# Order of the front stage, index keys and look-ups of a hybrid encoder step: six edits to one kernel

## The chip, the core and the metric

The kernel runs on one core of one Trainium2 chip. The metric is the time of one execution on the device in microseconds (us). The profile is one execution recorded by the hardware profiler; its engines are PE (TensorE matmul), PEld (TensorE weight load, beside PE), DVE (VectorE), ACT (ScalarE), POOL (GpSimd) and SP (SyncE, whose queue issues most of the DMAs, in order).

## The reference

One layer for two groups of tokens that share weights: 8 sequences of 16 sample tokens with 256 cached tokens each, and one prompt of 256 tokens; 384 rows of 1024 in all. Cut to what matters here:

```python
h = rmsnorm(x) * (1 + scale1) + shift1            # mod = silu(c) @ w_ada + b_ada, six rows of 1024 per sequence
P_rw, P_dsa, P_gate = split(h @ w_in)             # 3360, 3656 and 2048 columns
o_a = rwkv7(P_rw)                                 # recurrence with a state per head, 16 heads of 64
q, k, v, qi, ki, wi = split(P_dsa)                # qi: 8 heads of 64, ki: one of 64, wi: 8
score = sum_h wi[h] * relu(rope(qi[h]) @ rope(ki).T)
idx = top_k(score, min(256, L // 4))              # 64 or 68 keys per query
o_b = softmax_attention(q, k[idx], v[idx])
ga, gb = split(sigmoid(P_gate + b_gate))
m = ga * (o_a @ w_proj_a) + gb * (o_b @ w_proj_b)
x = x + gate1 * (m @ w_out)
h2 = rmsnorm(x) * (1 + scale2) + shift2
# PEER: per head two top-16 lists out of 128 keys, 16 best of their pair sums, expert number from the two lists
s1, i1 = top_k(s[..., 0, :], 16); s2, i2 = top_k(s[..., 1, :], 16)
sc, j = top_k(pair_sums(s1, s2), 16); e = take(i1 * 128 + i2, j)
x = x + gate2 * sum(softmax(sc) * gelu(peer_u[e] @ h2) * peer_v[e])
```

Outputs are the new x, the recurrence states, the shifted rows, and k, v, ki.

## The kernel before, in words

**Matmuls.** Most projections hold each weight chunk as a rounded high part and a low part (`hilo`, line 225: ScalarE writes the high part, VectorE or GpSimd the difference, as `lo_pattern` says), and the activations `LT` too, and add three products. `wload` (line 240) loads 512 KB pieces through a ring of four `w` buffers into four `wh` and three `wl`. `natp` (line 261) holds 128 tokens and streams weight columns: 24 matmuls per token tile of 128. `tposp` (line 273) holds weight columns and streams all 384 tokens: 24 matmuls for up to 128 columns, result transposed. Both write one of two PSUM banks named `mm`.

**The front stage** (`run`, line 1550) is a list of units in the order of the string `ORDER` (line 177): `G` a gate unit (line 1130: 128 columns of the gate projection, sigmoid, stored to DRAM in `gd`; units 0 to 7 are branch A's gates, 8 to 15 branch B's), `I` the index unit, `R` one of eight recurrence pairs (line 524: two heads, three projections, then a long chain of small steps on all engines, result stored to `oad`), `D` one of four attention quarters (line 914: four heads, result to `obd`), `M` a modulation unit (line 379: 256 columns of `silu(c) w_ada`, full float32, row `mr` stored to DRAM).

The string gives priorities, not the final order: the builder simulates a time line and puts on each engine's queue, and on SP's, the earliest ready instruction. Rings and PSUM banks still follow one another in the order of use. Tile memory is in pools that open and close as stacks: `rw` for the pairs on one side, on the other first `idx` for the index unit and, when that is done, `dsa` for the quarters in the same place. A tile waits for the readers and writers of what lay there before.

**The index unit** (`index`, line 878) projects `qi` (two units of 256 columns) and then `ki` with `wi` (72 columns), all with `natp` via `nat3` (line 871), rotates them, transposes them, and calls `index_s` (line 990, sample scores, cached keys brought by SP) and `index_p` (line 961, prompt scores). `select` (line 953) finds the best keys by rounds of `max` (eight values) and `match_replace`, 9 for the sample tokens and 8 for each of two prompt tiles, on VectorE. The masks `mks`, `mkp` are its results; they lie outside `idx`.

**The mix** (`mix`, line 1146) reads `obd` back in four pieces (`parts`, line 1137), makes gate B x projection B (8 x `tposp`), then the same for `oad` and branch A, adds, and goes on to `w_out`, the second norm and `h2`. Its pool opens over memory of the front stage.

**Expert selection** (`peer_select`, line 1257), called twice with four heads for the sample tokens and twice with eight for the prompt tiles, runs on VectorE: top-16 lists, then a look-up of the chosen index numbers. The look-up (lines 1313 to 1324) compares positions with 0..15 (bf16, 1024 elements per partition), multiplies with the numbers, and sums over 16 places; only one of the 16 is not zero. There are 12 of these. `dense_u` (line 1433, PE) and `peer_sparse` (line 1514, gathers on GpSimd and products on VectorE) run beside it and after it; then come the expert weights and the dense products up to the end.

Of the kernel before, what the change touches and what calls it, by code (L numbers as in the profile page):

```python
# [12 lines left out]
F32 = mybir.dt.float32  # L13
# [163 lines left out]
ORDER = "GGIRRDMMMGRMRDMRGMGGMRMDGMMRRMGDMMMGGGGGGMGGM"  # L177
# [15 lines left out]
class K:  # L193
# [171 lines left out]
    def mod_head(self):  # L365
        nc = self.nc
        cT = self.t([128, 8, 9], tag="cT")
        nc.sync.dma_start(cT, self.I["cT"])
        sg = self.t([128, 8, 9], tag="cS")
        self.sigmoid(sg, cT)  # L370
        self.st = self.fconst.tile([128, 8, 32], F32, name="cst")
        nc.vector.memset(self.st, 0.0)
        nc.vector.tensor_tensor(self.st[:, :, 0:9], sg, cT, op=OP.mult)
        self.bcol = self.fconst.tile([128, 16], F32, name="bcol")
        nc.sync.dma_start(self.bcol, self.I["b_col"])
        self.modd = self.dt_([128, 6144])
        self.scT = self.fconst.tile([128, 2, 8, 9], F32, name="scT")

    def mod_unit(self, u):
# [7 lines left out]
        mr = self.t([128, 256], tag="mr", pool=self.fill)  # L387
# [64 lines left out]
    def front_h(self):  # L452
# [6 lines left out]
        self.h1A = self.fconst.tile([128, 8, 9], F32, name="h1A")  # L459
# [418 lines left out]
    def index(self):  # L878
        nc = self.nc
        H = lambda t: t.rearrange("p i (h d) -> p i h d", d=64)  # L880
        qiTs = self.t([64, 8, 8, 16], tag="qiTs")
# [16 lines left out]
        kiT = self.t([128, NT], tag="kiT")  # L898
        x = self.t([128, 3, 72], tag="qx")
        self.nat3("ki", x, 72)  # L900
        kr = self.t([128, 3, 2, 64], tag="qr")
        self.rope(kr[:, :, 0:1], x[:, :, 0:64].unsqueeze(2), 0, 1)
        nc.gpsimd.tensor_copy(kr[:, :, 1], kr[:, :, 0])
        nc.sync.dma_start(self.O["ki"].rearrange("(i p) c -> p i c", p=128), kr[:, :, 0])
        wi = self.t([128, 3, 8], tag="wi")
        nc.scalar.activation(wi, x[:, :, 64:72], AF.Copy, scale=512 ** -0.5)
        p = self.ps([128, 3, 128], tag="dx")
        for i in range(3):
            nc.tensor.transpose(p[:, i], kr[:, i].rearrange("p a b -> p (a b)"), self.ident)
        nc.scalar.activation(kiT, p.rearrange("p i t -> p (i t)"), AF.Copy)  # L910
# [235 lines left out]
    def mix(self):  # L1146
# [3 lines left out]
        for br, (src, w, tg) in enumerate(((self.obd, "w_proj_b", "pb"), (self.oad, "w_proj_a", "pa"))):  # L1150
            LT = self.parts(src, tg)
            if br:
                mh, ml = self.mT = [self.t([128, 8, NT], F32R, tag=tag) for tag in ("pbh", "pbl")]
            for u in range(4):
                W = self.wload(I[w][:, u], 256)
                for c in range(2):
                    k = 2 * u + c
                    g = self.t([128, NT], tag="gm", bufs=2) if br else gb[:, k]
                    nc.sync.dma_start(g, self.gd[8 - 8 * br + k])
                    p = self.tposp(W, c, 128, LT)  # L1160
                    nc.vector.tensor_tensor(g, g, p, op=OP.mult)
                    if br:
                        nc.gpsimd.tensor_tensor(g, g, gb[:, k], op=OP.add)
                        self.hilo(mh[:, k], ml[:, k], g, eng="v")
# [92 lines left out]
    def peer_select(self, i, h0=0, nh=8):  # L1257
# [57 lines left out]
        for half in range(2):  # L1315
            for h in range(0, nh, 4):
# [7 lines left out]
                nc.vector.tensor_reduce(out=idx[:, half, hs], in_=oh.rearrange("p h c k -> p h k c"), op=OP.add, axis=AX.X)  # L1324
# [225 lines left out]
    def run(self):  # L1550
        self.dense = False
        with ExitStack() as front:
# [20 lines left out]
            with ExitStack() as s:  # L1573
# [4 lines left out]
                for x in ORDER:  # L1578
# [6 lines left out]
                    self.pool = rw if x == "R" else ds  # L1585
                    {"R": self.rwkv_pair, "M": self.mod_unit, "G": self.gate_unit, "D": self.dsa_quarter}[x](n[x])
# [117 lines left out]
```

## Time and profile before

| | us |
|---|---|
| median of three runs (1849.57 to 1854.88) | 1850.84 |
| the profiled execution | 1852.01 |
| its span, first to last instruction | 1850.2 |

| stretch (us) | what runs |
|---|---|
| 0 to 60 | norm, first 8 modulation units, head of the recurrence |
| 60 to 142 | index projections and scores, first pairs |
| 142 to 186 | selection of keys, pairs 0 and 1 |
| 186 to 745 | pairs, quarters, modulation and gate units |
| 745 to 897 | mix, output projection, second norm |
| 897 to 1090 | expert selection, first dense products |
| 1090 to 1350 | more dense products, weights of the experts |
| 1350 to 1850 | dense and gathered products up to the output |

The busy share of an engine is an average over stretches with different limits; TensorE's busy time counts pipelined matmuls, so a busy PE need not run at its peak. [...] In rows of instructions an arrow in brackets names what ended the idle time before.

### The profile page before, as it was taken

The numbers are of one execution on the slowest core, as the hardware profiler recorded it, in microseconds if no ns is written. First come the engines' busy times: TensorE is split into PE (matmuls) and PEld (weight loads), VectorE is DVE, ScalarE is ACT, GpSimd is POOL, SyncE is SP. The second block draws the span as 40 slices with busy tenths as digits, with TensorE's granted clock in tenths as the row PEclk, the third lists the DMA queues.
The fourth block names the chain that finished last, engine by engine and source line by source line (L and its number), as shares of the span: only waits on it lengthen the run. The fifth ranks groups of instructions, "written<-read, shape, count | busy, mean of one in ns | idle before, by whom it ended". The sixth has DMA issues, their size and how long they took to land. (4 is left out here: it accounts for less than half of the span.)

```text
span 1850.2 us, 33639 instructions
## 1 busy us (share of the span) xinstructions
PE 1736.5 (94%) x12621; PEld 1434.4 (78%) x12621; DVE 1372.4 (74%) x2922; ACT 702.0 (38%) x1412; POOL 684.7 (37%) x751
## 2 busy tenths in 40 slices
PE   7997999999999989899999889999999989999998
PEld 4995788877887868698877779999975556677765
DVE  4549677877777755444999998899967787787783
ACT  4422343333343333333412145478842222333332
POOL 2321233232232210023244534554346675555541
PEclk7987999999999989899999999999999999999999
DMA  8421472454364264745478988976489999999994
GB/s 310 140 79 28 133 257 75 150 170 124 104 206 144 88 209 134 253 140 193 161 291 311 337 295 304 394 269 221 160 293 373 395 372 372 336 378 352 334 355 147
DMA packets 181083, 434.11 MB, mean 235 GB/s; under 512 B 39348, under 2 KB 78388, under 8 KB 180920
## 3 DMA queue, kind: packets, MB, share of 16 engines
q1 hardware_dynamic: 144056, 297.73, 47.3%
q0 software_dynamic: 36864, 134.23, 19.4%
q8 instruction: 99, 1.62, 0.4%
q14 instruction: 64, 0.52, 0.1%
HBM read 401.65 MB, written 30.24 MB: 233 GB/s over the span
## 5 line engine op out<-in xcount | busy, mean ns | idle before, releaser
L231 DVE TENSOR_TENSOR wl<-w,wh 128x1024 fp32r<-128x1024 f32 x278 | 349.4, 1263 | 140.9 <-PE mm L223 67.8
L227 ACT ACTIVATE wh<-w 128x1024 fp32r<-128x1024 f32 x282 | 295.1, 1053 | 211.2 <-PE mm L223 88.4
L1524 POOL DMA_INDIRECT raw<-in_pu,pe x128 | 163.1, 1274 | 178.3 <-DVE acc L1545 42.5
L223 PE MATMUL fx<-h2h,wh 128*128 128x256 f32 x736 | 215.9, 293 | 6.7 <-ACT wh L227 3.1
L223 PE MATMUL fx<-h2h,wl 128*128 128x256 f32 x736 | 213.3, 290 | 6.0 <-DVE wl L231 5.8
L1524 POOL DMA_INDIRECT raw<-in_pv,pe x128 | 167.1, 1305 | 123.2 <-DVE raw L1535 45.6
L223 PE MATMUL fx<-h2l,wh 128*128 128x256 f32 x736 | 209.5, 285 | 0.0
L1535 DVE SCALAR_TENSOR_TENSOR raw<-raw,sh 128x1024 f32<-128x1024 f32 x128 | 161.3, 1272 | 28.6 <-DMA raw<-in_pu,pe 28.1
L1545 DVE SCALAR_TENSOR_TENSOR acc<-raw,dots,acc 128x1024 f32<-128x1024 f32 x127 | 166.3, 1310 | 12.0 <-DMA raw<-in_pv,pe 10.8
L223 PEld LDWEIGHTS fx<-h2h,wh 128*128 128x128 f32 x736 | 140.6, 191 | 12.9 <-ACT wh L227 4.4
L223 PEld LDWEIGHTS fx<-h2h,wl 128*128 128x128 f32 x736 | 139.9, 190 | 9.5 <-DVE wl L231 7.9
L223 PEld LDWEIGHTS fx<-h2l,wh 128*128 128x128 f32 x736 | 140.8, 191 | 2.1 <-issue 1.7
L223 PE MATMUL fx<-h2f,w 128*128 128x256 f32 x576 | 130.1, 387 | 11.4 <-ACT G L1451 10.2
L223 PEld LDWEIGHTS fx<-h2f,w 128*128 128x128 f32 x576 | 110.9, 194 | 28.9 <-ACT G L1451 11.4
L223 PE MATMUL mm<-LTh,wh 128*128 128x384 f32 (+1 forms) x344 | 122.9, 358 | 1.7 <-ACT wh L227 1.1
L223 PE MATMUL mm<-LTl,wh 128*128 128x384 f32 (+1 forms) x344 | 121.9, 354 | 1.0 <-POOL LTl L477 1.0
L223 PE MATMUL mm<-LTh,wl 128*128 128x384 f32 (+1 forms) x344 | 121.9, 354 | 0.8 <-DVE wl L231 0.8
L223 PE MATMUL mm<-wh,LTh 128*128 128x256 f32 (+1 forms) x360 | 105.7, 294 | 0.6 <-ACT qx L876 0.6
L223 PE MATMUL mm<-wh,LTl 128*128 128x256 f32 (+1 forms) x360 | 104.9, 291 | 0.0
L223 PE MATMUL mm<-wl,LTh 128*128 128x256 f32 (+1 forms) x360 | 104.6, 291 | 0.0
L1373 POOL TENSOR_TENSOR G<-G,wg 128x144 f32<-128x144 f32 (+1 forms) x64 | 55.7, 894 | 88.7 <-ACT wg L1370 88.7
L223 PEld LDWEIGHTS mm<-LTh,wh 128*128 128x128 f32 (+1 forms) x344 | 66.6, 194 | 10.1 <-issue 3.6
(552 smaller groups left out, 4186.0 us busy)
## 6 DMA issues: line engine op xcount, KB each, us to landing
w<-in_puT SPq DMA_DIRECT2D x128, 512.0 KB
w<-in_pv SPq DMA_DIRECT2D x128, 512.0 KB
w<-in_w_in SPq DMA_DIRECT2D x70, 512.0 KB
w<-in_w_ada SPq DMA_DIRECT2D x48, 512.0 KB
cKT<-in_cKT SPq DMA_DIRECT2D x32, 256.0 KB
cV<-in_cV SPq DMA_DIRECT2D x32, 256.0 KB
w<-in_w_pq SPq DMA_DIRECT2D x16, 512.0 KB
d<-wst SPq DMA_DIRECT2D x8, 832.0 KB
```

The source lines that it names most:

```text
L223: return self.nc.tensor.matmul(out, l, r, start=start, stop=stop, skip_group_check=True, **kw)
L227: self.nc.scalar.activation(hi, src, AF.Copy)
L231: (self.nc.vector if eng == "v" else self.nc.gpsimd).tensor_tensor(lo, src, hi, op=OP.subtract)
L1373: (nc.vector if w is p else nc.gpsimd).tensor_tensor(g, g, w[:, :, c0:c1], op=OP.mult)
L1524: d = nc.gpsimd.indirect_dma_start(out=u, out_offset=None, in_=src, in_offset=bass.IndirectOffsetOnAxis(ap=e[:, j:j + 1], axis=0))
L1535: nc.vector.scalar_tensor_tensor(u, u, 1.0, h2, op0=OP.mult, op1=OP.mult, accum_out=dots[:, j:j + 1])
L1545: nc.vector.scalar_tensor_tensor(acc, v, dots[:, j:j + 1], acc, op0=OP.mult, op1=OP.add)
```

## The change

Six edits:

1. Four gate units, written `g`, stand right after the index unit; one of the gates in the middle of the string and three of the six in a row near its end are gone. For `g` the low parts of the weights are made on GpSimd.
2. The index unit makes `ki` first, with one `tposp` (72 columns held, 384 tokens streamed), a copy, three transposes back and a copy, instead of three `natp`.
3. The modulation row `mr` has two buffers.
4. To make room, `bcol`, `scT` and `h1A` lie in the set-up pool, not in the constants that stay for the front stage.
5. The mix takes branch A first and branch B second.
6. The look-up adds the upper half of the 16 places to the lower in bf16, then the same with 8, and sums the remaining four with the reduce.

```diff
-ORDER = "GGIRRDMMMGRMRDMRGMGGMRMDGMMRRMGDMMMGGGGGGMGGM"
+ORDER = "GGIggggRRDMMMGRMRDMRGMGMRMDGMMRRMGDMMMGGGMGGM"
...
-        self.bcol = self.fconst.tile([128, 16], F32, name="bcol")
+        self.bcol = self.pool.tile([128, 16], F32, name="bcol")
...
-        mr = self.t([128, 256], tag="mr", pool=self.fill)
+        mr = self.t([128, 256], tag="mr", bufs=2, pool=self.fill)
...
     def index(self):
+        kiT = self.t([128, NT], tag="kiT")
+        W, n = self.win("ki")
+        kt = self.t([72, NT], tag="kt")
+        nc.scalar.activation(kt, self.tposp(W, 0, n, self.LT), AF.Copy)
+        x = self.t([128, 3, 72], tag="qx")
+        p = self.ps([128, 3, 72], tag="dx")
+        for i in range(3):
+            nc.tensor.transpose(p[:, i], kt[:, i * 128:(i + 1) * 128], self.ident[0:72, 0:72])
+        nc.scalar.activation(x, p, AF.Copy)
...
-        x = self.t([128, 3, 72], tag="qx")
-        self.nat3("ki", x, 72)
...
-        for br, (src, w, tg) in enumerate(((self.obd, "w_proj_b", "pb"), (self.oad, "w_proj_a", "pa"))):
+        for br, (src, w, tg) in enumerate(((self.oad, "w_proj_a", "pb"), (self.obd, "w_proj_b", "pa"))):
...
-                    nc.sync.dma_start(g, self.gd[8 - 8 * br + k])
+                    nc.sync.dma_start(g, self.gd[8 * br + k])
...
-                nc.vector.tensor_reduce(out=idx[:, half, hs], in_=oh.rearrange("p h c k -> p h k c"), op=OP.add, axis=AX.X)
+                for c in (8, 4):
+                    nc.vector.tensor_tensor(oh[:, :, 0:c], oh[:, :, 0:c], oh[:, :, c:2 * c], op=OP.add)
+                nc.vector.tensor_reduce(out=idx[:, half, hs], in_=oh[:, :, 0:4].rearrange("p h c k -> p h k c"), op=OP.add, axis=AX.X)
...
                     self.pool = rw if x == "R" else ds
+                    self.lo_pattern = "g" if x == "g" else "v"
+                    x = x.upper()
```

The rest of the `ki` path (rotation, store, transposes to `kiT`) is moved with it, unchanged.

More of the change, by code (lines that the diff above doesn't have):

```diff
@@ L373, in mod_head @@
         nc.vector.tensor_tensor(self.st[:, :, 0:9], sg, cT, op=OP.mult)
-        self.bcol = self.fconst.tile([128, 16], F32, name="bcol")
+        self.bcol = self.pool.tile([128, 16], F32, name="bcol")
         nc.sync.dma_start(self.bcol, self.I["b_col"])
         self.modd = self.dt_([128, 6144])
-        self.scT = self.fconst.tile([128, 2, 8, 9], F32, name="scT")
+        self.scT = self.pool.tile([128, 2, 8, 9], F32, name="scT")
     def mod_unit(self, u):
@@ L458, in front_h @@
         self.h1B = self.scT[:, 0]
-        self.h1A = self.fconst.tile([128, 8, 9], F32, name="h1A")
+        self.h1A = self.pool.tile([128, 8, 9], F32, name="h1A")
         h = self.xT
@@ L880, in index @@
         H = lambda t: t.rearrange("p i (h d) -> p i h d", d=64)
+        kiT = self.t([128, NT], tag="kiT")
[7 more added lines that the diff above has]
+        nc.scalar.activation(x, p, AF.Copy)
+        kr = self.t([128, 3, 2, 64], tag="qr")
+        self.rope(kr[:, :, 0:1], x[:, :, 0:64].unsqueeze(2), 0, 1)
+        nc.gpsimd.tensor_copy(kr[:, :, 1], kr[:, :, 0])
+        nc.sync.dma_start(self.O["ki"].rearrange("(i p) c -> p i c", p=128), kr[:, :, 0])
+        wi = self.t([128, 3, 8], tag="wi")
+        nc.scalar.activation(wi, x[:, :, 64:72], AF.Copy, scale=512 ** -0.5)
+        p = self.ps([128, 3, 128], tag="dx")
+        for i in range(3):
+            nc.tensor.transpose(p[:, i], kr[:, i].rearrange("p a b -> p (a b)"), self.ident)
+        nc.scalar.activation(kiT, p.rearrange("p i t -> p (i t)"), AF.Copy)
         qiTs = self.t([64, 8, 8, 16], tag="qiTs")
@@ L897, in index @@
             nc.scalar.activation(qiTp[:, u * 2:u * 2 + 2], p.rearrange("p c i t -> p c (i t)"), AF.Copy)
-        kiT = self.t([128, NT], tag="kiT")
-        x = self.t([128, 3, 72], tag="qx")
-        self.nat3("ki", x, 72)
[L901 to L910, printed above, removed]
         self.mks = self.index_s(qiTs, kiT, wi[:, 0])
```

## The prediction

> **What bounds the kernel now.** I read the page first, then the engines by stretches, then the order of time in each stretch where TensorE is not full.
>
> ```profile
> span 1850.2 us, 33639 instructions
> PE 1736.5 (94%) x12621; PEld 1434.4 (78%) x12621; DVE 1372.4 (74%) x2922; ACT 702.0 (38%) x1412; POOL 684.7 (37%) x751
> PEclk7987999999999989899999999999999999999999
> ```
>
> TensorE (PE) is busy for 94% of the span, so the change can save only where PE idles, runs at the lower of its two clock levels, or does work that goes away. The clock row has a dip in slices 3 and 4. The stretches show where the loss lies (columns: length, busy us of PE, PEld, DVE, ACT, POOL, then the granted clock):
>
> ```profile
> 62.10:82.60 20.50, 20.50 (x169) 20.19 (x168) 9.69 (x11) 9.28 (x17) 3.35 (x4) 1.00 0.36 118
> 82.60:101.50 18.90, 18.90 (x103) 18.50 (x102) 5.91 (x6) 4.26 (x9) 5.05 (x5) 0.64 0.29 88
> 101.50:142.00 40.50, 40.50 (x224) 35.82 (x222) 19.50 (x42) 13.89 (x31) 12.62 (x37) 0.96 0.25 75
> 142.00:163.00 21.00, 18.30 (x115) 13.24 (x115) 18.57 (x77) 6.20 (x17) 3.33 (x6) 0.99 0.17 44
> 163.00:186.00 23.00, 14.53 (x63) 9.22 (x63) 22.70 (x90) 3.18 (x8) 2.77 (x6) 0.50 0.09 17
> 240.00:661.00 421.00, 414.00 (x4502) 340.34 (x4495) 309.64 (x801) 146.64 (x361) 124.89 (x206) 0.99 0.45 139
> 661.00:672.00 11.00, 5.21 (x59) 3.11 (x56) 3.62 (x14) 2.41 (x5) 1.88 (x3) 0.65 0.82 278
> 745.00:770.00 25.00, 18.48 (x76) 13.98 (x75) 8.02 (x12) 8.81 (x19) 0.00 (x0) 0.80 0.84 288
> 897.00:1090.00 193.00, 174.71 (x828) 149.22 (x827) 191.19 (x763) 47.02 (x89) 74.57 (x70) 0.96 0.79 280
> 1090.00:1350.00 260.00, 253.96 (x2122) 251.16 (x2122) 246.65 (x340) 177.63 (x390) 118.77 (x105) 1.00 0.75 271
> 1350.00:1850.00 500.00, 465.46 (x1935) 328.13 (x1933) 365.01 (x451) 157.47 (x248) 261.43 (x215) 0.98 0.91 339
> ```
>
> From 240 to 661 us PE is busy 414 of 421 us at full clock: that stretch lasts as long as its PE work. Losses stand at 82 to 101 (busy, mostly half clock), 142 to 186 (idle and half clock, VectorE, DVE, full), 661 to 672, 745 to 770, and 897 to 1090 (DVE 191 of 193 us). From 1350 us on the DMA engines are 91% busy; the change leaves that stretch alone, so whatever is won before shifts it whole.
>
> **Index keys transposed and first.** Before, the key projection (`ki`) runs 3 token tiles x 24 matmuls that stream 72 columns; PE's timeline (start us, length us, instruction) has them beside 384-column ones:
>
> ```profile
> 82.68 0.28 PE L223 MATMUL mm<-wl,LTh 128*128 128x72 f32 x1
> 82.79 0.28 PE L223 MATMUL mm<-wh,LTl 128*128 128x72 f32 x1
> 138.09 0.34 PE L223 MATMUL mm<-LTh,wh 128*128 128x384 f32 x1
> 138.26 0.34 PE L223 MATMUL mm<-LTl,wh 128*128 128x384 f32 x1
> ```
>
> [...] The change replaces that run by wide matmuls, like those of 62.1 to 82.6, at 1.00. Bounds: 3.4 us (the clock falls all the same) to 10.2 us. I take **8**, near the upper end, since the fall starts inside this run while PE is without a gap. `ki` also moves ahead of both `qi` units, so the index scores no longer wait for it after them.
>
> **Four gate units beside the selection.** From the timelines: the first and the last step of the selection (rounds of max and replace on DVE), the last projection matmul ahead of PE's hole and the first work behind it, with the idle time before it in brackets; then, of the gate results' tile, its DVE step (shortest, median and longest ns):
>
> ```profile
> 141.68 0.44 DVE L958 MAX8 m<-isc 128x8 f32<-128x276 f32 x1
> 185.60 0.28 DVE L986 TENSOR_SCALAR mkp<-isc 128x256 bf16<-128x256 f32 x1
> 153.51 0.28 PE L223 MATMUL mm<-wh,LTl 128*128 128x256 f32 x1
> 172.16 1.41 PE L223 MATMUL fx<-cfront,ra 128*128 128x2 f32 x6 [7.58 <-DVE ra L581]
> L431 DVE TENSOR_SCALAR gg<-gg x16: 344/359/361, 61.3 to 743.1; 128x384 f32<-128x384 f32 x16
> ```
>
> The first attention quarter's tiles take the memory of the index pool, so its first projection fills the two `mm` banks by 153.5 us and no further projection starts until the last mask at 185.6. From 142 to 186 PE idles 2.7 + 8.5 = 11.2 us, and its 14.5 us of work at clock 0.50 would take half: 7.3 us more, 18.5 us in all. A gate unit is 24 matmuls of 384 columns, 4.1 us; four are 16.4 us. Their results leave through ScalarE, a 0.36 us DVE step and the `fill` pool, so the index pool doesn't hold them. They stand in program order ahead of recurrence pairs 0 and 1, whose projections so move up to 16.4 us back, into the hole. PE work is only moved: the gain is the hole filled, 0 to 16.4 us (18.5 us can't be passed). The selection starts earlier by the `ki` step, which makes filling it harder, and pairs 0 and 1 bring DVE work later: I take **12**.
>
> The low parts of these four (weights minus their rounded part) go to GpSimd (POOL). The four such steps that the kernel has elsewhere, DVE's, and a pair of them side by side in the timelines:
>
> ```profile
> L231 POOL TENSOR_TENSOR wl<-w,wh x4: 2372/2401/2884, 865.4 to 886.4; 128x1024 fp32r<-128x1024 f32 x4
> L231 DVE TENSOR_TENSOR wl<-w,wh 128x1024 fp32r<-128x1024 f32 x278 | 349.4, 1263 | 140.9 <-PE mm L223 67.8
> 882.04 2.88 POOL L231 TENSOR_TENSOR wl<-w,wh 128x1024 fp32r<-128x1024 f32 x1 [2.72 <-ACT wh L227]
> 882.96 3.05 DVE L231 TENSOR_TENSOR wl<-w,wh 128x1024 fp32r<-128x1024 f32 x1 [0.22 <-ACT wh L227]
> ```
>
> 4 x 2.4 = 9.6 us on POOL, which is busy 12.6 of 40.5 us there; queued behind each are the pairs' subtractions, the rotary products and the memset of the index weights, at most 2.4 us late. DVE loses 4 x 1.26 = 5 us of work in a stretch it does not bound. So nothing either way, if the low parts run while DVE has room (19.5 of 40.5 us busy at 101 to 142). But the last row shows a price: a DVE subtract beside a POOL one took 3.05 us, not 1.26. [...] Cost: 0 to 4 x 1.8 = 7 us; I take 0 and keep the rest as a rival.
>
> **Second row buffer for the modulation.** The timelines of ScalarE, the SP queue, PE and ScalarE again:
>
> ```profile
> 666.26 0.38 ACT L388 ACTIVATE mr<-mm 128x256 f32<-128x256 f32 x1 [6.72 <-DMA d<-mr]
> 660.38 0.43 SPq L396 DMA_DIRECT2D d<-mr  x1
> 667.26 0.90 PE L1105 MATMUL dx<-cfirst,se 128*128 128x128 f32 x3 [5.79 <-ACT se L1101]
> 670.50 1.06 ACT L227 ACTIVATE wh<-w 128x1024 fp32r<-128x1024 f32 x1 [2.88 <-DMA w<-in_w_in]
> ```
>
> With one row, ScalarE stood 6.72 us for the row's store, the softmax behind it stood too, and PE 5.79 us for that. A second row ends this. Late next is the weight transfer that ScalarE got only at 670.5, so part of the 11 us is refilled by that wait: 0 to 8 us (5.8 idle, about 2.6 of half clock); I take **4**. Its 1 KB per partition comes from three constants moved into the setup pool, all read for the last time there: nothing.
>
> **Swapped mix, fewer gates at the end.** A wait of the SP queue in 744 to 772 us, its stores of branch A's and branch B's last pieces, and the mix's first matmuls:
>
> ```profile
> SPq L1142 <- DMA d<-gg: 5.2, 1, 5.2
> 743.77 0.42 SPq L662 DMA_DIRECT2D d<-sq  x1
> 760.91 0.32 SPq L952 DMA_DIRECT2D d<-qr  x1
> 754.39 1.01 PE L223 MATMUL mm<-pbh,wh 128*128 128x384 f32 x2 [2.86 <-ACT pbh L227]
> ```
>
> Branch B's last piece is stored only at 760.9 and must be read back; branch A's last was stored at 743.8. With A first, B's tail has 8 x 24 x 0.17 = 33 us of matmuls over it. In 745 to 770 PE idles 6.5 us and half of its clock steps cost some 3.5 more: 0 to 10 us. The first load's 5.2 us wait for the last gate's store stays (the pool opens over the old one), so I take **6**. Of the four gates that leave, one stood in the middle and three stood before the mix, 12 us of cover for pair 7 and quarter 3. With A first, B's tail needs it no more, pair 7's might: 0 to 6 us lost, I take **-2**.
>
> **Look-ups halved.** Twelve each of the long reduce and of the 1024-element product, and the nearest short steps, by line:
>
> ```profile
> L1324 DVE TENSOR_REDUCE pix<-poh 128x64 f32<-128x1024 bf16 x12 | 23.8, 2018 | 0.0
> L1323 DVE TENSOR_TENSOR poh<-poh 128x1024 bf16<-128x1024 bf16 x12 | 7.9, 696 | 0.0
> L1327 DVE TENSOR_TENSOR pg<-pfv 128x64 f32<-128x64 f32 (+1 forms) x4 | 1.1, 275 | 0.0
> L1330 DVE TENSOR_REDUCE pgs<-pg 128x4 f32<-128x64 f32 (+1 forms) x4 | 1.1, 281 | 0.0
> ```
>
> A line from 275 ns (about 96 elements) to 696 (1024) gives 0.46 us for the 512-element add and 0.35 for the 256; one from 281 to 2018 ns gives 0.58 for the remaining reduce. 1.39 us instead of 2.02: 12 x 0.63 = 7.5 us of DVE. DVE is full in 897 to 1090, but some of it is gather arithmetic that only fills; PE idles 18.3 us there. -1 to 7.5 us (below nothing if gather steps slip between the three short ones); I take **4**.
>
> **Sum.** 8 + 12 + 4 + 6 - 2 + 4 = 32 us. The profiled execution took 1852.0 us, 1.8 over its span and 1.2 over the median of 1850.84: 1850.84 - 32 = **1819 us**.
>
> **Rivals.** *The hole only moves.* Pairs 0 and 1 come behind the gates, PE works the gates off while the scores are still being made, and idles again before the last mask. For: DVE is full at 163 to 186 whatever PE does. Against: the two pairs' projections, 2 x 3 x 24 x 0.17 = 24 us, then reach into the selection. The 12 goes: 1831 us.
>
> *The port price.* All four low parts fall on the DVE-bound selection, 4 x 1.8 = 7 us: 1826 us. [...] Against: ahead of the selection DVE is half idle, and the gates' weights load there.
>
> *Slower: the last pair becomes the mix's first wait.* A first means that pair 7 is needed when the mix begins; at 743.8 it was 6 us ahead of the first load. If the pairs form a chain without slack, pair 0 starts 16.4 - 8 us later, POOL's 9.6 us come on top, all pairs end up to 18 us later, and neither the hole nor the row buffer matters: the mix waits 12 us, the look-ups give 4 back: 1859 us. It decides once pair 7's store is issued after the last gate's. Against: PE is full from 240 to 661, so the pairs wait for PE rather than PE for them.
>
> *No effect.* The builder orders each queue by a simulated time; a new order may open new gaps as large as those closed: 1850 us.
>
> **Chances.** Forecast 0.55, hole moves 0.20, port price 0.10, slower 0.08, no effect 0.07. The first three are faster by more than 0.3% (5.6 us, about what a measurement here can tell): 0.85, same 0.07, slower 0.08. The upper bounds that stand together give 10 + 16 + 8 + 10 + 8 = 52 us, 1799; all at once is unlikely: low end 1803. The high end takes in the first two rivals and some 9 us more: 1840.
>
> **What would show it.** Right: granted clock near 1.00 over the `ki` stretch; PE idle under 4 us between the start of selection and the last mask, the last mask before 175 us; no ScalarE wait on `d<-mr`; first mix matmuls on `w_proj_a` without a second gap; the three look-up steps together near 1.4 us and the stretch to the last look-up shorter. Wrong: the idle block of PE before the last mask is still there, DVE subtracts of 3 us inside the selection, or PE waiting at the mix for branch A's last piece.

## The result, and the profile after

The changed kernel takes 1822.1 us (median of 4 runs, 1819.6 to 1824.4) beside 1852.7 us for the kernel before on the same chip: a ratio of 0.984, 95% interval 0.9805 to 0.9875. That is 30.6 us less, where 32 were predicted (1819, range 1803 to 1840). The number was right, by luck: the experiments show that several of its terms were not, and that the terms do not add.

The page of the changed kernel (profiled execution 1820.84 us): the span, the busy times, and the granted clock in 40 slices.

```profile
span 1819.1 us, 33550 instructions
PE 1722.2 (95%) x12576; PEld 1427.0 (78%) x12576; DVE 1353.9 (74%) x2942; ACT 701.7 (39%) x1411; POOL 687.8 (38%) x755
PEclk7998899999899998899999999999999999999999
```

PE is busy 14 us less than before (1736.5). The dip of the clock row in slice 3 (91 to 136 us) is gone. The one in slice 4 (136 to 182 us) is not, and it now reaches into slice 5. The same stretches as in the prediction (start and end, length, busy us and in brackets the instructions of PE, PEld, DVE, ACT and POOL, granted TensorE clock as a share of full speed, busy share of the DMA engines, GB/s):

```profile
82.60:101.50 18.90, 18.83 (x131) 18.06 (x130) 8.86 (x6) 7.43 (x12) 13.18 (x8) 1.00 0.36 110
...
142.00:163.00 21.00, 21.00 (x133) 17.32 (x131) 18.75 (x58) 3.88 (x10) 5.65 (x17) 1.00 0.26 82
163.00:186.00 23.00, 13.41 (x49) 8.24 (x48) 20.48 (x85) 6.67 (x16) 3.50 (x6) 0.54 0.07 11
...
661.00:672.00 11.00, 9.53 (x131) 6.78 (x131) 7.59 (x21) 5.58 (x12) 3.44 (x4) 1.00 1.00 361
745.00:770.00 25.00, 25.00 (x134) 23.08 (x133) 12.95 (x16) 10.62 (x14) 0.00 (x0) 1.00 0.57 188
725.00:750.00 25.00, 23.27 (x99) 18.93 (x99) 12.16 (x19) 10.24 (x19) 0.00 (x0) 0.73 0.70 243
```

The stretch that held the `ki` matmuls runs at 1.00 instead of 0.64 (`ki` itself is done before it now). The hole at 142 to 186 has moved back rather than closed: PE is full until 163, then as idle as before (13.4 of 23 us, clock 0.54), and the hole goes on past 186. The gap at 661 is closed. So is the one at 745, but the mix now starts 21 us earlier, and the last row (725 to 750, clock 0.73) shows a gap of its own there.

Tiles of the changed kernel: the first and last step of the selection, the first load of the mix, the gate units in the first 200 us (shortest, median and longest ns, first and last start).

```profile
L964 DVE MAX8 m<-isc x25: 274/410/451, 138.6 to 189.5; 128x8 f32<-128x276 f32 x9, 128x8 f32<-128x128 f32 x8, 128x8 f32<-128x256 f32 x8
L992 DVE TENSOR_SCALAR mkp<-isc x2: 211/242/272, 178.4 to 191.1; 128x128 bf16<-128x128 f32 x1, 128x256 bf16<-128x256 f32 x1
L1148 SPq DMA_DIRECT2D px<-d x8: 319/333/423, 729.0 to 750.4; - x8
L430 ACT ACTIVATE gg<-mm,hb x6: 557/562/580, 63.0 to 111.4; 128x384 f32<-128x384 f32 x6
```

The look-up's new steps in the changed kernel's groups by line, 872 to 1060 us (busy us, mean ns):

```profile
L1331 DVE TENSOR_TENSOR poh<-poh 128x512 bf16<-128x512 bf16 (+1 forms) x24 | 7.7, 350 | 0.0
L1332 DVE TENSOR_REDUCE pix<-poh 128x64 f32<-128x256 bf16 x12 | 6.6, 582 | 0.0
```

The last mask comes at 191.1, later than before (185.6), not ahead of 175. And the gates are not beside the selection at all: all six units of the front are through by 111.4, 27 us ahead of the first MAX8, and pairs 0 and 1 come behind them. PE's timeline of the changed kernel has the hole where it was:

```profile
179.88 0.87 PE L569 MATMUL fx<-cfirst,sq 128*128 128x128 f32 x3 [3.33 <-DVE TL L686]
187.45 1.41 PE L223 MATMUL fx<-cfront,ra 128*128 128x2 f32 x6 [6.70 <-DVE ra L581]
```

In the stage rows of both kernels the first row runs from the first MAX8 to the last mask, the second from there to the first load of the mix, the third from the last norm step to the last look-up. The kernel before:

```profile
141.70:185.60 43.90, 32.73 (x179) 22.38 (x176) 41.20 (x164) 9.51 (x26) 6.40 (x12) 0.74 0.13 30
185.60:750.10 564.50, 545.66 (x5929) 447.20 (x5927) 390.75 (x997) 197.70 (x474) 147.78 (x228) 0.98 0.48 151
895.00:1088.70 193.70, 175.41 (x827) 149.71 (x826) 191.89 (x763) 48.49 (x93) 73.63 (x69) 0.96 0.78 280
```

The changed kernel:

```profile
138.60:191.10 52.50, 41.05 (x212) 31.21 (x210) 47.47 (x168) 12.75 (x32) 9.78 (x24) 0.75 0.14 38
191.10:729.00 537.90, 529.97 (x5861) 437.44 (x5862) 386.80 (x1000) 193.13 (x464) 148.63 (x230) 0.98 0.49 154
872.60:1059.40 186.80, 173.39 (x819) 147.67 (x819) 184.30 (x787) 47.14 (x92) 69.85 (x70) 0.97 0.80 293
```

Up to the mask the change loses 5.5 us; from the mask to the mix it wins 26.6; to the norm 1.3; in the expert selection 6.9; behind it 1.8. Together 31.1 us of span. PE's idle time in the selection is 52.5 - 41.05 = 11.45 us; it was 11.17. VectorE's work there grew from 41.20 to 47.47 us (three weight subtracts, 3.7 us, of which there was none, and other steps of the pairs between those of the selection), and the selection takes 52.5 us instead of 43.9.

**How far one execution can be read.** The kernel before was executed 80 times beside the experiments, with medians of 1850.3 to 1855.2 us on the chips, and single times from 1838.75 us (granted clock 0.970) to 1863.27 (0.960). Time and mean granted clock go together (correlation -0.84, some 16 us for 0.010 of clock). So the verdicts below stand on the ratios with their intervals, and a single profile serves to show where things lie, not differences of 5 us. An example bears on what follows: the first gate unit's ScalarE step starts at 60.7 us in the kernel before, at 63.0 in the changed kernel's profile, and at 60.3 to 61.2 in the profiles of three kernels below that differ from the changed one only behind it (all but the swap, all but the gates, low parts on VectorE). The changed kernel's profile is thus some 2 us late before the four gates begin, and where it matters times are counted from that step. A difference of two ratios is given in us of 1851; kernels on different chips are compared only so.

### The profile page after: what moved, and what is told of

The parts are those of the page before. It is cut to its first block, busy times and chain, and to the rows that moved or that the text cites. A ratio compares the mean times of both kernels' runs of the same rounds, so it can differ in the third digit from the quotient of the medians.

```text
span 1819.1 us, 33550 instructions
## 1 busy us (share of the span) xinstructions
PE 1722.2 (95%) x12576; PEld 1427.0 (78%) x12576; DVE 1353.9 (74%) x2942; ACT 701.7 (39%) x1411; POOL 687.8 (38%) x755
## 5 line engine op out<-in xcount | busy, mean ns | idle before, releaser
L231 DVE TENSOR_TENSOR wl<-w,wh 128x1024 fp32r<-128x1024 f32 (+1 forms) x274 | 343.9, 1258 | 140.3 <-ACT wh L227 77.2
L227 ACT ACTIVATE wh<-w 128x1024 fp32r<-128x1024 f32 (+1 forms) x282 | 296.0, 1053 | 203.9 <-PE mm L223 75.1
L1553 DVE SCALAR_TENSOR_TENSOR acc<-raw,dots,acc 128x1024 f32<-128x1024 f32 x127 | 164.9, 1298 | 10.5 <-DMA raw<-in_pv,pe 9.2
L1543 DVE SCALAR_TENSOR_TENSOR raw<-raw,sh 128x1024 f32<-128x1024 f32 x128 | 157.6, 1242 | 14.4 <-DMA raw<-in_pu,pe 14.2
L223 PE MATMUL mm<-LTh,wh 128*128 128x384 f32 (+2 forms) x352 | 124.5, 354 | 1.6 <-ACT wh L227 1.0
L223 PE MATMUL mm<-LTh,wl 128*128 128x384 f32 (+2 forms) x352 | 123.2, 350 | 0.6 <-DVE wl L231 0.6
L223 PE MATMUL mm<-LTl,wh 128*128 128x384 f32 (+2 forms) x352 | 121.7, 346 | 1.1 <-POOL LTl L477 1.1
L223 PE MATMUL mm<-wh,LTh 128*128 128x256 f32 x336 | 99.1, 295 | 0.0
L223 PE MATMUL mm<-wl,LTh 128*128 128x256 f32 x336 | 98.3, 293 | 0.0
L223 PE MATMUL mm<-wh,LTl 128*128 128x256 f32 x336 | 98.1, 292 | 0.0
L223 PEld LDWEIGHTS mm<-LTh,wh 128*128 128x128 f32 (+2 forms) x352 | 66.6, 189 | 10.1 <-issue 5.2
```

Source lines behind the costliest of these rows:

```text
L223: return self.nc.tensor.matmul(out, l, r, start=start, stop=stop, skip_group_check=True, **kw)
L227: self.nc.scalar.activation(hi, src, AF.Copy)
L231: (self.nc.vector if eng == "v" else self.nc.gpsimd).tensor_tensor(lo, src, hi, op=OP.subtract)
L1543: nc.vector.scalar_tensor_tensor(u, u, 1.0, h2, op0=OP.mult, op1=OP.mult, accum_out=dots[:, j:j + 1])
L1553: nc.vector.scalar_tensor_tensor(acc, v, dots[:, j:j + 1], acc, op0=OP.mult, op1=OP.add)
```

## The experiments

The theory after the result: the gain is the sum of its parts, as predicted, though the hole was not filled. The rivals: one part carries all; or the parts are links of one chain up to the mix, so that none pays alone. All ratios are against the kernel before on the same chip.

### Four parts alone

**Gates alone**, the edit:

```diff
-ORDER = "GGIRRDMMMGRMRDMRGMGGMRMDGMMRRMGDMMMGGGGGGMGGM"
+ORDER = "GGIggggRRDMMMGRMRDMRGMGMRMDGMMRRMGDMMMGGGMGGM"
+                    self.lo_pattern = "g" if x == "g" else "v"
+                    x = x.upper()
```

> The kernel before with one part of the change: the four gate units in front of pairs 0 and 1, their low parts on GpSimd. Theory A (the gates fill part of the hole, 12 us in the prediction): the last mask, at 185.6 us before, comes by 195 (16.4 us of gate matmuls go in, most of them where PE stood), the first load of the mix 16 us earlier relative to it, time about 1840 us, PE idle from the first MAX8 to the last mask under 6 us. Theory B (the hole only moves, 0 us): the last mask comes near 185.6 + 16.4 = 202, the idle block ahead of the mask is as long as before (8 us or more, at half clock), time 1850 us within 4.

Measured: 1853.8 us, ratio 1.0006 (0.9979 to 1.0033). The last mask came at 183.8, as theory A had it, and the first load of the mix at 747.9 all the same. The two stage rows of this kernel:

```profile
137.60:183.80 46.20, 40.11 (x236) 33.00 (x234) 42.57 (x151) 15.33 (x36) 13.95 (x32) 0.87 0.23 66
183.80:747.90 564.10, 542.36 (x5874) 439.63 (x5875) 394.79 (x1024) 192.60 (x464) 153.14 (x234) 0.96 0.48 147
```

Here the gates do fill part of the hole: PE idles 6.1 us from the first MAX8 to the last mask instead of 11.2, at clock 0.87 instead of 0.74. But the stretch behind the mask is as long as before (564.5), though 16 us of gate matmuls have left it: PE idles 22 us there, and the clock is 0.96, where the changed kernel has 8 us and 0.98. Theory A held up to the mask, theory B in the time alone; neither held whole.

**Keys alone** (`ki` through `tposp`, three transposes, ahead of the `qi` units, as in the change).

> The kernel before with the index keys alone: transposed, wide matmuls, ahead of the query units. Theory A (the key run costs 3.4 us of work and 6.8 us of clock, and PE sets when the scores begin): granted clock near 1.00 from 62 to 140 us, first MAX8 and last mask 6 to 10 us earlier than 141.7 and 185.6, time about 1842 us. Theory B (the time won is lost again ahead of the mask, because the first attention quarter and the pairs are waited for at the same places as before): last mask earlier, but the idle block behind it or the first gap after it as much longer, time 1847 to 1851. Theory C (the clock falls in that place whatever runs there, since the fall belongs to the stretch and not to the narrow matmuls): clock 0.64 to 0.8 again over 82 to 101, last mask 3 to 4 us earlier, time 1847.

Measured: 1850.9 us, ratio 1.0000 (0.9981 to 1.0019). Granted clock 1.00 from 62 to 142 us, last mask 179.2: the place works as in theory A and theory C is out. The time does not move, as in theory B. Three views of this kernel say where it goes. A wait of the SP queue around the mix:

```profile
SPq L1148 <- DMA d<-mr: 6.7, 1, 6.7
```

The engines from 725 to 750 us:

```profile
725.00:750.00 25.00, 15.72 (x86) 11.70 (x85) 9.18 (x16) 7.83 (x18) 0.00 (x0) 0.75 0.73 232
```

PE's timeline, the first matmuls of the mix:

```profile
745.99 1.01 PE L223 MATMUL mm<-pbh,wh 128*128 128x384 f32 x2 [6.92 <-DMA px<-d]
```

The first load of the mix was issued only when the store of the last modulation row had landed (issued at 734.0), and PE stood 6.9 us for it.

**Second row alone** (`bufs=2` for `mr`, three constants in the setup pool).

> The kernel before with the second modulation row alone (its memory from the three constants moved to the setup pool). Theory A: ScalarE's two waits for the row's store (12.1 us together) go, PE's 5.8 us idle at 661 to 672 and its half clock go with the longer one, time 1843 to 1848 us. Theory B (what stood behind the row finds the next wait, the weight transfer that ScalarE got only at 670.5): the gap at 661 to 672 is there with another cause, time 1850 within 3.

Measured: 1854.7 us, ratio 1.0017 (0.9994 to 1.0040): nothing gained, as in theory B. ScalarE's waits for the row's store are gone, but the gap at 661 to 672 is still there (PE busy 6.06 of 11 us, before 5.21), and PE's timeline shows its new cause, a weight transfer:

```profile
671.18 1.08 PE L223 MATMUL mm<-w,cst 128*32 128x256 f32 x8 [4.34 <-DMA w<-in_w_ada]
```

**Look-ups alone**:

```diff
-                nc.vector.tensor_reduce(out=idx[:, half, hs], in_=oh.rearrange("p h c k -> p h k c"), op=OP.add, axis=AX.X)
+                for c in (8, 4):
+                    nc.vector.tensor_tensor(oh[:, :, 0:c], oh[:, :, 0:c], oh[:, :, c:2 * c], op=OP.add)
+                nc.vector.tensor_reduce(out=idx[:, half, hs], in_=oh[:, :, 0:4].rearrange("p h c k -> p h k c"), op=OP.add, axis=AX.X)
```

> The kernel before with the halved look-ups alone: two bf16 adds of 512 and 256 elements ahead of a reduce of 256. In the changed kernel the three steps take 0.35 + 0.35 + 0.58 = 1.28 us (24 adds of mean 350 ns, 12 reduces of 582 ns) instead of 2.02, 12 x 0.74 = 8.8 us of VectorE. Theory A (VectorE bounds the expert selection): last look-up reduce relative to the last h2 step 6 to 9 us earlier, time 1842 to 1845 us. Theory B (part of VectorE's work there only fills, and gather steps slip between the three short steps): 0 to 4 us, 1847 to 1851.

Measured: 1840.1 us, ratio 0.9946 (0.9922 to 0.9970), 10 us. The stretch from the last norm step to the last look-up, 193.7 us before:

```profile
896.60:1081.80 185.20, 174.53 (x818) 148.71 (x817) 184.25 (x787) 47.46 (x92) 69.66 (x70) 0.96 0.82 296
```

8.5 us shorter, nearly all of VectorE's saving (12 x 0.74 = 8.8): theory A. It is the only part that pays by itself.

**Swap alone**:

```diff
-        for br, (src, w, tg) in enumerate(((self.obd, "w_proj_b", "pb"), (self.oad, "w_proj_a", "pa"))):
+        for br, (src, w, tg) in enumerate(((self.oad, "w_proj_a", "pb"), (self.obd, "w_proj_b", "pa"))):
```

> The kernel before with the mix swap alone (branch A first). Theory A (6 us in the prediction, less the wait for the last gate): the first load of the mix stays near 745 to 750 us, since it waits for the last gate's store, and branch B's last store (760.9) lies under branch A's matmuls; PE idle in the 25 us after the first load falls from 6.5 to 2 us or less, time 1842 to 1847 us. Theory B (interaction: the swap pays only when the gates have left the end, because here the gates at the end already cover branch B): time 1850 within 3.

Measured: 1852.0 us beside 1855.2, ratio 0.9998 (0.9971 to 1.0024): theory B. (Its profile, 1843.5 us, was the fastest of its ten runs: the clock was 0.82 over 82 to 101 there, where the kernel before, with the same instructions up to the mix, had 0.64.)

So alone the parts give 10 us (look-ups) and four times nothing; together they give 30.

### One part left out

**All but the swap**, the changed kernel with branch B first:

> The changed kernel with the mix in its old order (branch B first). By the terms of the prediction this costs 6 us: 1828. Theory B (interaction: with the gates alone the last mask stayed at 183.8 with 16 us more done in front of it, yet the first load of the mix came only at 747.9 and branch B's last store at 762.2, so what the gates gave in front was lost at the mix; the swap is what cashes it): 10 to 18 us, 1832 to 1840, and the first load of the mix 8 to 18 us later than 729.0. Theory C (the gates and the keys pay without it): 1820 to 1826.

Measured: 1820.6 us, ratio 0.9813 (0.9775 to 0.9852) against the changed kernel's 0.9840 (0.9805 to 0.9875); first load of the mix at 728.0. Theory C: no gain from the swap is seen in company either.

**All but the gates**, with the order of units of before:

> The changed kernel with the order of units of before (no gates beside the selection, none on GpSimd). By the prediction's terms the gates are worth 12 - 2 = 10 us: 1832. Theory B (the gates alone gave nothing, but with the swap they do): 1832 to 1838. Theory C (their place doesn't matter even then, and the rest of the gain is in keys, rows, swap and look-ups together): 1820 to 1826; then the stretch from the last mask to the first load of the mix is as long as in the kernel before (564 us) but its end earlier by the keys and the swap.

Measured: 1831.8 us, ratio 0.9877 (0.9838 to 0.9916) against the changed kernel's 0.9840 (0.9805 to 0.9875): 7 us, with intervals that overlap. That is at theory B's lower end and at the prediction's own 1832, and the overlap leaves it open whether the gates pay with their low parts on GpSimd. Against the run with all low parts on VectorE (0.9793, below), which differs from this one by the gates alone, it is 16 us with intervals just apart: the gates do pay in company. The two stage rows:

```profile
135.30:179.20 43.90, 34.05 (x172) 22.01 (x173) 41.84 (x172) 12.79 (x33) 3.25 (x7) 0.65 0.10 19
179.20:740.80 561.60, 544.23 (x5900) 449.87 (x5896) 385.05 (x983) 195.72 (x468) 149.18 (x228) 0.97 0.49 152
```

Against this the changed kernel's four gates cost 191.1 - 179.2 = 11.9 us up to the mask (some 9 counted from the first gate unit's step, 63.0 and 60.3) and give back 561.6 - 537.9 = 23.7 behind it. That is how they can pay without filling the hole.

**All but the keys**:

> The changed kernel with the index keys as before (three narrow natural-order products behind the query units). By the prediction's terms 8 us: 1830; granted clock 0.64 again over the narrow run. The keys alone brought the last mask 6.4 us and the first load of the mix 8.9 us earlier in the profile, though the median time did not move. Theory B (interaction: time won in front counts only when the end of the two branches can use it, as it can here): 1828 to 1832, last mask 6 to 10 us later than 191.1. Theory C (the keys are worth nothing): 1820 to 1824.

Measured: 1836.7 us, ratio 0.9920 (0.9892 to 0.9948), 15 us. Clock 0.64 again over 82 to 101. Its last mask, 186.0, is not later but 5 us earlier than 191.1; in its profile the loss is behind it, 567 us to the mix instead of 538. (That profile, 1849.1 us, is one of the slowest of ten runs with a median of 1836.7, so it shows the place of the loss better than its size.) The price is larger than theory B's and in another place.

**All but second row and swap**:

> The kernel before with three of the five parts: gates, keys and look-ups, without the second row and without the swap. Theory A (the second row and the swap are worth nothing even in company; the three carry all): 1822 us within 4, first load of the mix at 729 within 4. Theory B (the row's 4 us and the swap's share are there in company): 1828 to 1834. Theory C (gates and keys each gave nothing alone, and only the row or the swap lets them pay): 1838 to 1842, what the look-ups give alone.

Measured: 1839.3 us, ratio 0.9930 (0.9903 to 0.9957): theory C. Since leaving out the swap costs nothing, the row (with the three constants moved for it) that gave nothing alone is worth some 17 us here (0.9930 - 0.9840; 22 against all but the swap). The stores of the last five modulation rows (first and last start) in this kernel, with one row:

```profile
L396 SPq DMA_DIRECT2D d<-mr x5: 327/369/392, 667.0 to 723.6; - x5
```

The same in all but the swap, with two rows:

```profile
L396 SPq DMA_DIRECT2D d<-mr x5: 326/432/467, 657.8 to 708.4; - x5
```

With one row the last unit is stored 15 us later, and the mix begins 11.5 us later (739.5, not 728.0). Between the two runs lies one row, and the mix's order that did nothing.

### What the chain is

GpSimd's timeline has one `gnv` step at the end of each pair. First and last of the eight, in the kernel before:

```profile
L425 POOL TENSOR_TENSOR gnv<-rs,mhalf x8: 1314/1334/2242, 239.8 to 732.9; 128x6 f32<-128x6 f32 x8
```

Keys alone:

```profile
L425 POOL TENSOR_TENSOR gnv<-rs,mhalf x8: 1331/1336/1972, 220.2 to 713.6; 128x6 f32<-128x6 f32 x8
```

Gates alone:

```profile
L425 POOL TENSOR_TENSOR gnv<-rs,mhalf x8: 1331/1333/2772, 265.8 to 736.3; 128x6 f32<-128x6 f32 x8
```

The changed kernel:

```profile
L425 POOL TENSOR_TENSOR gnv<-rs,mhalf x8: 1332/1336/1543, 253.8 to 718.4; 128x6 f32<-128x6 f32 x8
```

| kernel | last pair | first load of the mix | between |
|---|---|---|---|
| before | 732.9 | 750.1 | 17.2 |
| keys alone | 713.6 | 741.2 | 27.6 |
| gates alone | 736.3 | 747.9 | 11.6 |
| all but the gates | 724.5 | 740.8 | 16.3 |
| all but the keys | 740.4 | 753.1 | 12.7 |
| all but row and swap | 724.0 | 739.5 | 15.5 |
| all but the swap | 717.5 | 728.0 | 10.5 |
| changed | 718.4 | 729.0 | 10.6 |

The keys bring the pairs forward by 19 us, and then the modulation units at the end are what the mix waits for (the 6.7 us above). The gates shorten that end by 5.6 us, but send pair 0 back by 26 us, so that the last pair is 3 us later than before. The second row lets the modulation units at the end go through. Each part alone moves one of the things that the mix needs, and the others hold it: that is the reading that fits. It rests on single profiles, though the ratios agree with it. Why pair 0, 26 us late with the gates alone, makes up all but 3 us by the last pair is not settled; nor is why the last pair comes 11 us later in all but the gates than with the keys alone, where the first came at the same time (220.7 and 220.2).

### Where the low parts go, and the hole once more

**Low parts on VectorE**, the changed kernel with

```diff
-                    self.lo_pattern = "g" if x == "g" else "v"
+                    self.lo_pattern = "v"
```

> The changed kernel with the four low parts on VectorE instead of GpSimd. In its trace GpSimd's four ran at 80.0 to 97.7 us, 2.4 us each, where VectorE was busy 9.5 of 19 us. Theory A (nothing either way, as the prediction took it): 1822 within 3, four subtracts of 1.2 to 1.3 us on VectorE there. Theory B (they would push VectorE's work in the selection back): last mask 2 to 5 us later, 1825 to 1828. Theory C (the port price is in the changed kernel, hidden in longer VectorE steps): 2 to 7 us faster.

Measured: 1811.1 us, ratio 0.9793 (0.9756 to 0.9830), 9 us less than the changed kernel, with intervals that overlap from 0.9805 to 0.9830: theory C's direction, past its upper end, but the size is not settled. The timelines of VectorE and GpSimd in the changed kernel:

```profile
79.97 2.40 POOL L231 TENSOR_TENSOR wl<-w,wh 128x1024 fp32r<-128x1024 f32 x1 [3.98 <-ACT kiT L899]
80.47 2.72 DVE L868 TENSOR_TENSOR qr<-qx,rt 128x768 f32<-128x768 f32 x1 [1.14 <-ACT qx L876]
82.32 1.74 POOL L865 TENSOR_TENSOR rpt<-qx,rt 128x384 f32<-128x384 f32 x1
...
90.25 2.40 POOL L231 TENSOR_TENSOR wl<-w,wh 128x1024 fp32r<-128x1024 f32 x1 [0.66 <-PE mm L223]
90.70 2.77 DVE L868 TENSOR_TENSOR qr<-qx,rt 128x768 f32<-128x768 f32 x1 [4.68 <-ACT qx L876]
```

VectorE's timeline with all low parts on VectorE:

```profile
79.06 1.77 DVE L868 TENSOR_TENSOR qr<-qx,rt 128x768 f32<-128x768 f32 x1
...
89.30 1.76 DVE L868 TENSOR_TENSOR qr<-qx,rt 128x768 f32<-128x768 f32 x1
```

Both rotary products of the queries run beside a GpSimd subtract and take 1 us more; a third step, `qr` at 95.35, takes 3.13 instead of 0.96. And GpSimd's own rotary products, which the queries need, queue behind the low parts. The 1.77 us need not be an undisturbed time either: in the kernel before the same two steps take 1.77 and 1.76 us (at 73.38 and 83.92) and end 0.82 and 0.80 us behind a rotary product of GpSimd's, as the three long steps of the changed kernel end 0.81 to 0.82 us behind its subtracts.

How much of the 9 us this explains is another matter. First MAX8 comes at 135.6 instead of 138.6, last mask at 183.9 instead of 191.1, the mix at 723.3 instead of 729.0. But the first gate unit's step is at 60.8 instead of 63.0, so only 0.8 of the 3 us up to the first MAX8 lie behind it. The rest of the gain up to the mask is inside the selection, 48.3 us instead of 52.5, where no gate's low part is made on GpSimd in either kernel. VectorE's queue has another order there, and in the changed kernel, on its timeline, it waits twice for PE, which runs at half clock (0.50 over 168 to 173 us):

```profile
168.60 0.42 DVE L611 TENSOR_TENSOR MKp<-fx,cfront 128x256 f32<-128x256 f32 x1 [1.31 <-PE fx L223]
171.42 0.42 DVE L558 TENSOR_SCALAR kk<-Xk,cols 128x384 f32<-128x384 f32 x1 [1.02 <-PE fx L620]
```

From the mask to the mix, and from there to the end, the two profiles are alike within 2 us. So the lengthened steps are shown, and that the kernel is faster without them is likely; that they are its cause is not shown. The edit also changes the order of the queues, and the six runs had a mean granted clock of 0.971 to 0.979, the changed kernel's four 0.965 to 0.969.

**Seven gates behind the pairs**, their low parts on GpSimd:

```diff
-ORDER = "GGIggggRRDMMMGRMRDMRGMGMRMDGMMRRMGDMMMGGGMGGM"
+ORDER = "GGIRRgggggggDMMMRMRDMRMMRMDGMMRRMGDMMMGGGMGGM"
```

> The changed kernel with the gates behind the projections of pairs 0 and 1 instead of ahead of them, and seven of them (three more taken from the middle of the order). In the changed kernel the four ran at 63 to 111 us, before the first MAX8 (138.6), and PE still idled 11 us and ran at half clock from 166 to 194. Theory A (place decides: gates as the last work in front of the attention quarter fill the hole itself): last mask by 185 with 12 us more gate work behind it, PE idle between 160 and the last mask under 5 us, clock over 0.8 there, time 1805 to 1814. Theory B (VectorE bounds the selection, and pairs 0 and 1 then load it at the same time whatever PE does; the hole moves once more, or the middle misses its three gates as cover): last mask at 190 or later, or new gaps between 250 and 700, time 1820 to 1830.

Measured: 1816.0 us, ratio 0.9822 (0.9787 to 0.9857). Its two stage rows:

```profile
135.00:188.00 53.00, 47.42 (x277) 40.69 (x275) 50.65 (x161) 19.19 (x38) 15.46 (x12) 0.94 0.36 106
188.00:722.30 534.30, 522.57 (x5795) 424.14 (x5794) 377.96 (x988) 187.38 (x457) 148.23 (x228) 0.98 0.47 151
```

The hole is half filled (5.6 us idle, clock 0.94 instead of 0.75), with three gates more done by a mask that is no later than in the changed kernel (188.0 and 191.1; 127.7 and 128.1 us behind the first gate unit's step). So place does matter: behind the pairs, gates go into the hole. But mask and time miss theory A (185, 1805 to 1814), and 12 us less gate work behind the mask shortens that stretch by 3.6 us only. Against the changed kernel it is 3 us, well inside the intervals. VectorE is busy 50.65 of 53 us, partly for this reason, in its timeline beside GpSimd's:

```profile
136.01 0.34 DVE L987 SCALAR_TENSOR_TENSOR isc<-rel,wi,isc 128x128 f32<-128x128 f32 x1
...
137.35 2.54 DVE L987 SCALAR_TENSOR_TENSOR isc<-rel,wi,isc 128x128 f32<-128x128 f32 x1
137.36 2.38 POOL L231 TENSOR_TENSOR wl<-w,wh 128x1024 fp32r<-128x1024 f32 x1 [6.93 <-PE mm L223]
...
145.53 2.37 POOL L231 TENSOR_TENSOR wl<-w,wh 128x1024 fp32r<-128x1024 f32 x1 [5.05 <-PE mm L223]
...
145.72 0.43 DVE L965 MATCH_REPLACE8 isc<-m,isc 128x276 f32<-128x276 f32 x1
146.07 1.85 DVE L684 TENSOR_TENSOR TX<-TL,NL 48x4 f32<-48x4 f32 x1
```

A step of four elements takes 1.85 us and ends when GpSimd's ends, 147.9. A replace step passes beside the same subtract at its usual 0.43 us.

**Seven gates, low parts on VectorE**: `ORDER = "GGIggggRRgggDMMMRMRDMRMMRMDGMMRRMGDMMMGGGMGGM"` with `lo_pattern = "v"`.

> The changed kernel with seven gates in front, four ahead of pairs 0 and 1 as in the change and three behind them, all low parts on VectorE, three gates taken from the middle of the order. Joins what two runs showed: low parts on VectorE 1811 us with the hole still there (last mask 183.9, PE idle and at half clock behind 160), and seven gates behind the pairs 1816 us with the hole nearly filled but VectorE's steps beside GpSimd's longer (128x16 step 2.4 us, gate step 0.68 instead of 0.36). Theory A (hole and ports are separate prices): the three gates add 3 x (1.26 + 0.36) = 4.9 us of VectorE work to the selection and 12.3 us of PE work into the hole: last mask near 189, clock over 0.8 from 160 to 189, no VectorE step lengthened, time 1801 to 1807. Theory B (the middle misses the gates, as the 527 to 534 us from the mask to the mix seemed to say): 1808 to 1816. Theory C (VectorE bounds the selection, three more low parts push it): last mask at 195 or later, 1812 or more.

Measured: 1824.6 us, ratio 0.9865 (0.9836 to 0.9893); 1812.7 to 1831.1, the profiled run the fastest of the six. Its two stage rows:

```profile
136.40:187.60 51.20, 46.23 (x273) 38.34 (x271) 46.89 (x159) 17.29 (x38) 11.01 (x24) 0.97 0.29 81
187.60:724.70 537.10, 523.11 (x5799) 429.73 (x5800) 384.11 (x1009) 186.13 (x458) 147.99 (x230) 0.97 0.49 150
```

The hole is half closed here too (5.0 us idle), at clock 0.97, and no gate's subtract on GpSimd is left beside a step of VectorE. Yet the stretch behind the mask is 537 us long for 12 us less gate work than in the run with low parts on VectorE (539). Filling the hole with gates from the middle gains nothing; by the ratios, 0.9865 and 0.9793 with intervals apart, it loses 13 us. The best of the six runs is in theory B's range, the median behind it; the last mask at 187.6 speaks against C. Why the other five runs are up to 18 us longer, no profile of them shows. Seven gates behind the pairs with low parts on VectorE was not run. By its median the best version is the changed kernel with all low parts on VectorE, 1811 us.

## Why the prediction was right, and where it was not

- **Keys, 8 us.** What was expected of the clock held: it stayed at 1.00 where it had fallen to 0.64. (Whether it went with the narrow shape or with its place behind the queries is not separated: the edit changes both.) No run shows the 8 us, or its bounds of 3.4 and 10.2 us, as such; the traces have in their place 72 narrow matmuls and 12 others from 82.6 to 96.5 us in the kernel before, and in the changed kernel 24 wide ones that start within 66.4 to 70.4, 0.17 us apart, at granted clock 1.00 (62 to 84). Alone it gave nothing, left out it cost 15 us. The step "whatever is won before shifts it whole" failed for the part alone, since the modulation units at the end became the late ones; with the row and the gates they are not.
- **Gates, 12 - 2 us.** About 7 us is what they are worth in company as built, some 16 with their low parts on VectorE, but not by the hole. "PE work is only moved: the gain is the hole filled" is the step that failed: alone they half filled the hole and gained nothing, in company PE idled in it as long as before (11.45 and 11.17 us). What was taken too lightly is "pairs 0 and 1 bring DVE work later": with the gates VectorE had 47.47 us of work in the selection instead of 41.84 without them, and the selection took 52.5 us instead of 43.9. The rival "the hole only moves" was right about the place; its price, the whole 12 us gone, was wrong: the four gates cost some 9 to 12 us in front and gave back 23.7 behind.
- **Low parts on GpSimd, 0 us.** Probably a mis-sized term: some 9 us by the ratios, above its bound of 7, but with overlapping intervals. The rival had longer steps right and the place wrong: the steps lengthened were the queries' rotary products, ahead of the selection. "A stretch it does not bound" looked at VectorE's busy share, not at who waits for the step. In the profiles only 0.8 us shows at the first MAX8, and some 4 us more lie in the selection, in another order of VectorE's queue; where the rest comes from stays open. What the two engines share, no run shows: behind the name "port price" stand steps of VectorE that took longer beside a GpSimd subtract, 3.05 instead of 1.26 us at 882.96 in the kernel before, and the 1.85 us step that ends 0.02 us behind GpSimd's.
- **Second row, 4 us.** Alone 0, in company some 17. The wait for the row's store went as said; the gap at 661 closed only in company, since alone the next weight transfer held PE there, the lower bound of the prediction. The larger effect, that two rows let the last modulation units through 15 us earlier, was not in the sum.
- **Swap, 6 us.** No gain seen, alone or in company. The cover for branch B's tail was read from one gap; when the pairs and the fill units end earlier, the gap lies around the first load instead (715 to 745: PE busy 27.2 of 30 us at clock 0.66, with branch B first 26.8 at 0.66), and it is there in either order.
- **Look-ups, 4 us.** 10 us. The durations were close (0.70 + 0.58 = 1.28 us against an estimated 1.39), but "some of it is gather arithmetic that only fills" took half of 7.5 us away; 8.5 of 8.8 us showed in the stretch.
- **The sum.** 32 against 30.6 us came out because errors cancelled: the swap's 6 us were not there and the gates gave 7 instead of 10, while the look-ups gave 6 more and the keys and the row gave more than their terms. And it is no sum: left out one at a time, gates, keys and row cost 7, 15 and 17 us, with 10 for the look-ups (alone; they were not left out) 49 us of a gain of 30.6. The forecast treated as independent what depend on one another up to the mix. That is its main failing, and the right number does not mend it.

The signs named in the prediction: the clock over `ki`, no wait on `d<-mr` and the three look-up steps came as "right"; PE's hole and the time of the last mask as "wrong"; the first mix matmuls are on branch A, but with a gap ahead of them. The slower rival's sign came too: pair 7's store is issued at 724.1, 15 us after the last gate's, and the first load's last wait is for that store; but it is 1.8 us long, not 12. The gates make the last pair later than in the kernel before only in the runs without early keys (736.3 and 740.4 instead of 732.9), and there the gates alone give nothing, without that rival's 9 us of loss.

## What to carry to other kernels

Where a list of units is reordered by a builder, a unit put "beside" a stall can run well before it, as the gates did here: look which work is queued behind it, and on which engines, since that is what moves into the stall, or past it. Gains ahead of a joint pay only as far as everything that the joint waits for comes earlier; list these (last pair, last unit, last store) with their times, and price each part against the next late one, before adding. A helper engine's free time may be no free place: look at the other engine's steps beside its instruction (2.72 instead of 1.77 us here), and price the order of the queues that changes with it.

## What the runs showed of the hardware

In the kernel before, PE's granted clock averaged 0.64 of full speed from 82.6 to 101.5 us, a stretch in which the profile shows PE busy 18.9 of 18.9 us. The trace has two values of it, 1.00 and 0.50. It was 1.00 when the run of 72-column matmuls began at 82.6 us and up to 87, 0.72 from 87 to 88, 0.50 from 88 to 101, past the end of that run, and 0.96 from 101 to 102, under 384-column matmuls. The spacing went with it: the 72-column matmuls start 0.11 us apart at 1.00 and 0.21 at 0.50, the 384-column ones 0.32 at 0.50 and 0.17 at 1.00. PE's timeline across the fall:

```profile
87.25 0.28 PE L223 MATMUL mm<-wh,LTh 128*128 128x72 f32 x1
87.95 0.41 PE L223 MATMUL mm<-wl,LTh 128*128 128x72 f32 x1
```

In all six kernels that have this run behind the queries the clock averaged 0.58 to 0.82 over 82 to 101 us, after 1.00 over 62 to 82. With the wide `ki` matmuls ahead of the queries it was 1.00 over 82 to 101, or over a longer stretch around it, in seven of eight kernels; of the eighth, seven gates behind the pairs, stands an average of 0.97 over 76.7 to 135.0. The 0.82 (swap alone) came with the same instructions up to the mix as the 0.64. Over 80 executions of one kernel the mean granted clock lay between 0.958 and 0.970, and the time was the shorter, the higher it was (correlation -0.84).

Beside a GpSimd subtract of 2.4 to 2.7 us several of VectorE's steps took longer. In the seven gates behind the pairs a step of four float32 elements took 1.85 us, where one took 0.15 in the changed kernel, and ended 0.02 us behind the subtract; a score step took 2.54 instead of 0.33 and ended 0.15 us behind it; a 16-element step took 2.38 instead of 0.17 in the changed kernel. A replace step took its usual 0.43 there.
